# A planner's clock set to measured durations, and a DeltaNet front that may start beside the norm of the block two before

## The chip, the cores and the metric

The kernel runs on one core of a Trainium2 chip. The metric is the device time of one execution in microseconds, from start to end on that core; lower is better. Times of a profile come from one execution taken by the hardware profiler.

## The reference, cut to what matters

One layer of a hybrid encoder for two request groups with the same weights: a new stream of 16 meta tokens and 1024 frames, and a running stream of 64 frames. D_MODEL is 2048, and everything is float32.

```python
xn = _rmsnorm(h, norm_w)
proj = jnp.einsum('bld,dp->blp', xn, w_in)                 # 2048 x 8208
a_b, a_c, a_x, a_z, qkv, z_b, b_logit, a_logit = jnp.split(proj, PROJ_CUTS, axis=-1)
u_full = jnp.concatenate([conv_a_prev.astype(dt), a_c * a_x], axis=1)
y_a = a_b * _causal_conv(u_full, conv_a_w) * jax.nn.silu(a_z)          # mixer A, width 3
qkv_c = jax.nn.silu(_causal_conv(qkv_full, conv_qkv_w)).astype(f32)    # mixer B, width 4
# q, k normalised per head (8 heads of 128); beta = sigmoid(b); g = -exp(a_log) * softplus(a + dt_bias)
# gated delta rule in chunks, exact WY form:
a_mat = jnp.where(strict, kk, 0.0) + eye
t_mat = lax.linalg.triangular_solve(a_mat, eye, left_side=True, lower=True, unit_diagonal=True)
v_new = u_i - w_i @ s;  o = q_i exp(g_i) @ s + qk_i @ v_new;  s = s exp(g_last) + k_i.T @ v_new
o = _rmsnorm(o, o_norm_w) * jax.nn.silu(z_b)
y = jnp.einsum('blm,md->bld', jnp.concatenate([y_a, y_b], axis=-1), w_out)   # 2048 x 2048
return h + y                                               # then a final rmsnorm
```

## The kernel before, in words

**Tiles and stages.** The 1104 tokens lie in three pieces of 336, 384 and 384 columns (`PIECES`), and 9 chunks of 128 columns for the delta rule, three in a piece. A float32 product is three passes of the one-pass type `fp32r`: the tensor and the weight are each split into a high and a low part (`xh`, `xl`, `wh`, `wl`), and high times high, low times high and high times low are summed in PSUM. ScalarE makes `wh` (a cast), VectorE makes `wl` (a subtraction).

- Up to about 250 us: the input is loaded, normed and split while the first jobs run.
- To about 1843 us: the **jobs**. A job (`project`, line 427 and on) is 128 columns of `w_in` for all three pieces: 16 steps of k, each nine matmuls of 320 to 384 columns, into three of the four PSUM buffers `pj`. Weights come in four chunks of four k (`Weights.get`). After each k it calls `pump`. When a job is done, `post` has VectorE read its PSUM out (`raw`, `cs`, `xt`, `za`, `ya`, `zr`) and puts the rest of its convolution in a queue, `convs`. The jobs of a head of mixer B are k, q, v, z; of mixer A c, x, z, b. They come in the order b0 b1 b2 b3 a2 b4 a3 b5 a4 b6 b7 a5 a6 a7, after a0 and a1.
- Beside the jobs: the **DeltaNet** blocks, 24 of them (8 heads, 3 pieces; `NG`). `dn_front` (line 772) loads `kq`, transposes q and k (`psq`, `psk`), norms them, makes the masks `bm` and `at`, multiplies (`psm`, one for each chunk), and hands `bm` to GpSimd, which inverts 32x32 triangles in a loop of 60 instructions and returns them through DRAM in `t32` (in the trace `t`). `dn_back` (line 858) completes the inverse (`psx`, `psy`), then for each of the three chunks forms `r`, `u` and the new state (`psr`, `psu`, `psn`, `po`), then norms the output (`so`, `ro`, `on`), transposes it (`pot`) and gates it (`zg`). The small matmuls are float32, two instructions each.
- From 1843 us: `w_out`, in blocks of 512 columns (`po`), residual, norm, stores.

**What sets the order.** VectorE's and TensorE's instructions go out in the order in which the program writes them, apart from matmuls that the framework moves forward where a PSUM buffer isn't free in its own estimate. The program finds the order with a clock of its own, `clk`, in planned microseconds: `mm` and `tr` add to `pe`, and the wrapper `Timed` (line 46) adds to `dve` and `act`, from whichever is later, TensorE's clock or the engine's own. A generator's `yield d` makes its next step due at the largest of the three clocks plus `d` (`step`, line 174); `pump` (line 183) runs every due step, one front and one back at a time, and then lets convolution steps out while VectorE's clock is less than 0.7 ahead:

```python
        while convs and clk["dve"] - clk["pe"] < 0.7:
            if not step(convs[0]):
                convs.popleft()
```

`flush_convs` writes out what is left of them at the end of a job, before `post`. A front starts when the one before is done and `f - b <= 1`, where `b` counts finished backs; a back starts when `el_done` of its block, the planned end of GpSimd's solve, is reached. The front sets that at its end:

```python
        pool_free[0] = el_done[3 * h + p] = max(clk["pe"] + EL[0], pool_free[0]) + EL[1]
```

In the back, the loop over chunks (line 911 and on) ends with `yield 0.2`; the norm follows in the same step as the end of the loop, then `yield 3.2`, then `pot` and `zg`. Before the last job (line 1047 and on) the program runs `pump` without matmuls until all 24 backs are done.

SP's queue issues the loads and most stores, in program order: weights (`Weights.load`, line 232), `kq` (line 776), `bm` to DRAM (line 841).

Of the kernel before, what the change touches and what calls it, by code (L numbers as in the profile page):

```python
# [8 lines left out]
F32 = mybir.dt.float32  # L9
# [8 lines left out]
P = 128  # L18
# [7 lines left out]
NG = 3 * NH  # L26
# [40 lines left out]
def hymba_kernel(ctx: ExitStack, tc: tile.TileContext, hT, x_prompt, x_sample, w_in, w_ba, w_out, cst1, cst2, par,  # L67
                 s_delta, fnw, y_p, y_s, o_ca, o_cq, o_dp, o_ds):
    nc = tc.nc
    clk = {"pe": 0.0, "dve": 0.0, "act": 0.0}  # L70
    V = Timed(nc.vector, clk, "dve", 0.09, 0.00104)
    S = Timed(nc.scalar, clk, "act", 0.2, 0.00083)
    G, T, Q = nc.gpsimd, nc.tensor, nc.sync

    def mm(out, lhsT, rhs, start, stop):
        n = 1
        for d in rhs.shape[1:]:
            n *= d
        if lhsT.dtype == F32R:
            clk["pe"] += max(n / 2400 + 0.003, 0.107)  # L80
        else:
            clk["pe"] += 4 * max(n, lhsT.shape[1]) / 2400
        T.matmul(out, lhsT, rhs, start=start, stop=stop)  # L83

    def tr(out, in_, idn):
# [53 lines left out]
    def rsqrt(y, t, v):  # L139

        V.tensor_scalar(t.bitcast(I32), v.bitcast(I32), 1, None, ALU.logical_shift_right)
        V.tensor_scalar(y.bitcast(I32), t.bitcast(I32), -1, 0x5F3759DF, ALU.mult, ALU.add)
        for _ in range(3):
            V.tensor_tensor(t, y, y, ALU.mult)
            V.scalar_tensor_tensor(t, t, -0.5, v, ALU.mult, ALU.mult)
            V.scalar_tensor_tensor(y, t, 1.5, y, ALU.add, ALU.mult)

# [20 lines left out]
    gens = []  # L168
    done = set()
    fronts, backs, el_done, front_of, state = [0], [0], {}, {}, {}  # L170
    running = {}
    pool_free = [0.0]

    def step(it):

        try:
            d = next(it[1])
        except StopIteration:
            return False
        it[0] = max(clk.values()) + (d or 0.0)  # L180
        return True

    def pump():
        while True:
            moved = False
            f, b = fronts[0], backs[0]
            if "gate" in done and "front" not in running and f < NG and f - b <= 1:
                h, p = divmod(f, 3)
                if (KQ, h, p) in done and (QQ, h, p) in done:
                    running["front"] = [0.0, dn_front(h, p)]  # L190
            if "back" not in running and b < f and b < NG and el_done.get(b, 1e9) <= clk["pe"]:
                h, p = divmod(b, 3)
                if (VQ, h, p) in done and (ZQ, h, p) in done:
                    running["back"] = [0.0, dn_back(h, p)]
            for k in list(running):
                if running[k][0] <= clk["pe"]:
                    moved = True
                    if not step(running[k]):
                        del running[k]
                        if k == "back":  # L200
                            backs[0] += 1
                        elif k == "front":
                            fronts[0] += 1
            if not moved:
                break
# [3 lines that stand above are left out]
# [6 lines left out]
    class Weights:  # L215
# [20 lines left out]
        def split(self):  # L236
# [5 lines left out]
            wl = self.room(self.n_split, "l")  # L242
            V.tensor_tensor(wl, wr, wh.bitcast(F32), ALU.subtract)
            self.out.append((wh, wl))
# [209 lines left out]
    with ExitStack() as pro:  # L454
# [80 lines left out]
        a, n = PIECES[0]  # L535
# [108 lines left out]
    with ExitStack() as pro:  # L644
# [10 lines left out]
        for p in range(3):  # L655
            a, n = PIECES[p]
# [99 lines left out]
    dn = net.enter_context(tc.tile_pool(name="dn", bufs=1))  # L756
# [3 lines left out]
    def tmp(name, tag, bufs, shape=(P, 3, P)):  # L760
        return dn.tile(list(shape), F32, tag=tag, name=name, bufs=bufs)

    def psd(name):
        return pd.tile([P, 4, P], F32, tag="pd", name=name)

    EL = (5.0, 45.0)
    t32 = [dn.tile([P, 3, P], F32, tag=f"t32_{i}", name=f"t32_{i}") for i in range(2)]
    for i in range(2):
        V.memset(t32[i], 0.0)
# [2 lines left out]
    def dn_front(h, p):  # L772

        kq = tmp("kq", "kq", 2, (P, 3, 2, P))
        for i, w in ((0, KQ), (1, QQ)):
            Q.dma_start(kq[:, :, i, :], scr[h][w][p].rearrange("p (c t) -> p c t", t=P))
        gr = tmp("gr", "gr", 1)
        r0 = h * NCH + 3 * p
        Q.dma_start(gr, gscr[None, r0:r0 + 3, :].to_broadcast([P, 3, P]))
        yield 2.1  # L780
        c3 = slice(3 * p, 3 * p + 3)
        ss = dn.tile([P, 6], F32, tag="ss", name="ss", bufs=2)
        jk = dn.tile([P, P], BF16, tag="jk", name="jk")
        pq_ = psd("psq")
        for c in range(3):
            tr(pq_[:, c, :], kq[:, c, 1, :], ident)
        for c in range(3):
            S.activation(jk, pq_[:, c, :], AF.Square, accum_out=ss[:, 3 + c:4 + c])
        yield 0.0
        pk_ = psd("psk")  # L790
        for c in range(3):
            tr(pk_[:, c, :], kq[:, c, 0, :], ident)
        for c in range(3):
            S.activation(jk, pk_[:, c, :], AF.Square, accum_out=ss[:, c:c + 1])
        V.tensor_scalar(ss, ss, 4 * EPS, None, ALU.add)
        rq = rsqrt_of(dn, ss, 6, "rq")


        cq = dn.tile([P, 12], F32, tag="cq", name="cq", bufs=2)
        V.tensor_scalar(cq[:, 0:3], rq[:, 3:6], float(P) ** -0.5, None, ALU.mult)  # L800
        V.tensor_tensor(cq[:, 3:6], hb[:, h, c3], rq[:, 0:3], ALU.mult)
        V.tensor_tensor(rq[:, 3:6], rq[:, 0:3], rq[:, 0:3], ALU.mult)
        V.tensor_tensor(cq[:, 6:9], nbeg[:, h, c3], rq[:, 3:6], ALU.mult)
        V.tensor_tensor(cq[:, 9:12], nb[:, h, c3], rq[:, 3:6], ALU.mult)
        kn = tmp("kn", "kn", 2)
        V.tensor_tensor(kn, pk_[:, 0:3, :], kds[:, h, c3, None].to_broadcast([P, 3, P]), ALU.mult)
        km = None
        if p == 0:
            km = dn.tile([P, P], F32, tag="km", name="km")
            V.tensor_scalar(km, pk_[:, 0, :], kdm[:, h:h + 1], None, ALU.mult)  # L810
        yield 0.0

        bm = tmp("bm", "bm", 2)
        for c in range(3):
            cc = 3 * p + c
            V.scalar_tensor_tensor(bm[:, c, :], gr[:, c, :], gc[:, h, cc:cc + 1], cst[:, C_MS:C_MS + P], ALU.subtract,
                                   ALU.max)
        S.activation(bm, bm, AF.Exp, scale=-1.0)
        at = tmp("at", "at", 2)
        for c in range(3):  # L820
            cc = 3 * p + c
            V.scalar_tensor_tensor(at[:, c, :], gr[:, c, :], gc[:, h, cc:cc + 1], cst[:, C_MT:C_MT + P], ALU.subtract,
                                   ALU.min)
        S.activation(at, at, AF.Exp)
        S.activation(gr, gr, AF.Exp)
        if p == 0:

            V.memset(bm[64:P, 0, 0:64], 0.0)
            V.memset(at[0:64, 0, 64:P], 0.0)
        yield 0.0  # L830
        for c in range(3):
            pm = psd("psm")
            mm(pm[:, 0:2, :], kq[:, c, 0, :], kq[:, c, :, :], True, True)
            V.scalar_tensor_tensor(bm[:, c, :], pm[:, 0, :], cq[:, 9 + c:10 + c], bm[:, c, :], ALU.mult, ALU.mult)
            V.tensor_tensor(at[:, c, :], pm[:, 1, :], at[:, c, :], ALU.mult)
            yield 0.0
        yield 1.4

        eT = dn.tile([12, 32, 32], F32, tag="eT", name="eT", bufs=1)
        i = (3 * h + p) % 2  # L840
        Q.dma_start(whole(e_in[i]), bm)
        G.dma_start(eT, blocks(e_in[i]))  # L842
        tm = dn.tile([12, 240], F32, tag="tm", name="tm", bufs=1)
        for j in range(1, 31):
            n = 31 - j
            t = tm[:, 0:n * j].rearrange("m (i r) -> m i r", r=j)
            G.tensor_tensor(t, eT[:, j + 1:32, j:j + 1].to_broadcast([12, n, j]),  # L847
                            eT[:, j:j + 1, 0:j].to_broadcast([12, n, j]), ALU.mult)
            G.tensor_tensor(eT[:, j + 1:32, 0:j], eT[:, j + 1:32, 0:j], t, ALU.add)  # L849
        G.dma_start(blocks(e_out[i]), eT)  # L850
        G.dma_start(t32[i], whole(e_out[i]))
        yield 0.3

        V.tensor_tensor(kq[:, :, 1, :], kq[:, :, 1, :], gr, ALU.mult)
        front_of[h, p] = (kq, kn, km, at, cq, bm)
        pool_free[0] = el_done[3 * h + p] = max(clk["pe"] + EL[0], pool_free[0]) + EL[1]

    def dn_back(h, p):
        kq, kn, km, at, cq, bm = front_of.pop((h, p))
# [51 lines left out]
        for c in range(3):  # L911
# [31 lines left out]
            mm(po[:, c, :], kq[:, c, 1, :], s, False, True)  # L943
            state[h] = sn
            yield 0.2
        if p == 2:
            Q.dma_start(o_dp[h], state[h])

# [308 lines left out]
```

## Time and profile before

| | us |
|---|---|
| median of 3 runs | 2252.47 (2252.29 to 2257.59) |
| the profiled execution | 2251.76 |
| its span, first to last instruction | 2250.0 |
| TensorE busy | 2188.0 |
| VectorE busy | 1361.8 |
| GpSimd busy | 875.4 |
| ScalarE busy | 602.4 |

The granted clock of TensorE was 0.994 of full speed over the span. A busy time counts instructions that run, without waits for semaphores; ends of matmuls are modelled by the profiler. "Idle before" is the time for which an engine stood ahead of a group of instructions, and the name behind it is what ended that.

### The profile page before, as it was taken

How to read it: one execution, taken by the hardware profiler on the slowest of the kernel's cores; microseconds unless marked ns; L12 is line 12 of the kernel's file. 1: busy time of each engine (PE TensorE's matmuls, PEld its weight loads, DVE VectorE, ACT ScalarE, POOL GpSimd, SP SyncE). 2: the span in 40 equal slices, each digit the busy share in tenths (PEclk: the TensorE clock that was granted, in tenths of full speed). 3: DMA queues.
4: the chain of work that ended last, by engine and by line, in shares of the span. 5: the costliest groups of instructions: out<-in, count | busy, mean ns of one | idle time of the engine just before them, and what ended most of it. 6: DMA issues, size and time to landing. Idle time of an engine off the chain costs nothing. (4 is left out here: it accounts for less than half of the span.)

```text
span 2250.0 us, 35424 instructions
## 1 busy us (share of the span) xinstructions
PE 2188.0 (97%) x12794; PEld 2071.4 (92%) x12794; DVE 1361.8 (61%) x3540; ACT 602.4 (27%) x1483; POOL 875.4 (39%) x1516
## 2 busy tenths in 40 slices
PE   8999999999999999999999999999999999999997
PEld 8999899999999999999999999999999997788886
DVE  6653475777585556665775567675645345474644
ACT  7232121222222212212222222222221125444341
POOL 0000038475556566666657655657473000000000
PEclk9999999999999999999999999999999999999999
DMA  7223132222222122223232223232221228664652
GB/s 262 78 87 94 39 92 81 84 86 89 84 88 81 56 81 88 81 59 90 72 99 64 81 75 87 85 87 78 72 74 53 94 82 279 207 198 145 225 166 85
DMA packets 162067, 231.12 MB, mean 103 GB/s; under 512 B 17756, under 2 KB 89636, under 8 KB 161764
## 3 DMA queue, kind: packets, MB, share of 16 engines
q1 hardware_dynamic: 156356, 217.30, 31.2%
q0 software_dynamic: 3072, 7.11, 1.7%
q10 hardware_dynamic: 2464, 4.46, 0.5%
q8 instruction: 100, 1.64, 0.3%
q14 instruction: 75, 0.61, 0.1%
HBM read 184.61 MB, written 44.17 MB: 102 GB/s over the span
## 5 line engine op out<-in xcount | busy, mean ns | idle before, releaser
L83 PE MATMUL pj<-xh,wh 128*128 128x384 f32 x2048 | 694.9, 340 | 11.5 <-DVE raw L61 3.9
L83 PE MATMUL pj<-xl,wh 128*128 128x384 f32 x2048 | 692.4, 338 | 1.3 <-DVE xl L61 1.3
L83 PE MATMUL pj<-xh,wl 128*128 128x384 f32 x2048 | 691.3, 338 | 0.0
L61 DVE TENSOR_TENSOR wl<-wr,wh 128x512 fp32r<-128x512 f32 x464 | 335.5, 725 | 343.6 <-ACT wh L61 341.0
L83 PE MATMUL pj<-x,wh 128*128 128x320 f32 (+3 forms) x2048 | 519.2, 333 | 6.6 <-ACT x L61 6.6
L61 ACT CAST wh<-wr 128x512 fp32r<-128x512 f32 x464 | 285.8, 618 | 845.5 <-PE pj L83 626.7
L847 POOL TENSOR_TENSOR tm<-eT 12x30 f32<-12x30 f32 (+4 forms) x720 | 399.6, 555 | 121.7 <-DMA eT<-e_in 67.1
L849 POOL TENSOR_TENSOR eT<-eT,tm 12x30 f32<-12x30 f32 (+4 forms) x720 | 422.9, 587 | 56.4
L83 PEld LDWEIGHTS pj<-xh,wh 128*128 128x128 f32 x2048 | 387.2, 189 | 17.3 <-DVE xt L61 4.8
L83 PEld LDWEIGHTS pj<-xl,wh 128*128 128x128 f32 x2048 | 387.0, 189 | 2.9 <-DVE xl L61 2.2
L83 PEld LDWEIGHTS pj<-xh,wl 128*128 128x128 f32 x2048 | 386.8, 189 | 0.0
L83 PEld LDWEIGHTS pj<-x,wh 128*128 128x128 f32 x2048 | 349.3, 190 | 12.6 <-ACT x L61 6.7
L83 PE MATMUL pj<-x,wl 128*128 128x320 f32 (+3 forms) x1024 | 320.4, 313 | 5.2 <-DVE wl L61 5.2
L842 POOL DMA_DIRECT2D eT<-e_in x24 | 17.2, 716 | 578.2 <-DMA wr<-in_w_in 310.8
L83 PE MATMUL po<-wh,yh 128*128 128x512 f32 x656 | 238.9, 396 | 1.6 <-DVE yh L61 1.5
L83 PE MATMUL po<-wl,yh 128*128 128x512 f32 x528 | 208.9, 396 | 1.8 <-DVE wl L61 1.7
L83 PEld LDWEIGHTS pj<-x,wl 128*128 128x128 f32 x1024 | 193.3, 189 | 7.1 <-DVE wl L61 6.6
L83 PEld LDWEIGHTS po<-wh,yh 128*128 128x128 f32 x656 | 123.1, 188 | 32.9 <-DVE yh L61 2.7
L61 DVE SCALAR_TENSOR_TENSOR acc<-raw,pk,acc 128x384 f32<-128x384 f32 (+1 forms) x216 | 147.1, 681 | 6.0
L83 PE MATMUL po<-wh,yl 128*128 128x512 f32 x336 | 132.8, 395 | 0.0
L83 PEld LDWEIGHTS po<-wl,yh 128*128 128x128 f32 x528 | 99.1, 188 | 27.5 <-DVE wl L61 4.0
L61 ACT ACTIVATE raw<-acc 128x384 f32<-128x384 f32 (+1 forms) x72 | 36.8, 512 | 154.2 <-DVE acc L61 154.2
(242 smaller groups left out, 2127.9 us busy)
## 6 DMA issues: line engine op xcount, KB each, us to landing
wr<-in_w_in SPq DMA_DIRECT2D x288, 256.0 KB, 3.1
wr<-in_w_out SPq DMA_DIRECT2D x176, 256.0 KB, 2.8
scr<-acc SPq DMA_DIRECT2D x48, 192.0 KB, 1.9
kq<-scr SPq DMA_DIRECT2D x48, 192.0 KB, 3.0
hres<-in_x_prompt SPq DMA_DIRECT2D x32, 256.0 KB, 5.4
yr<-yscr SPq DMA_DIRECT2D x32, 192.0 KB, 3.7
scr<-co SPq DMA_DIRECT2D x24, 192.0 KB, 2.4
gr<-gscr SPq DMA_DIRECT2D x24, 192.0 KB, 3.5
```

What stands on the lines that cost most here:

```text
L61: return fn(out, *a, **k)
L83: T.matmul(out, lhsT, rhs, start=start, stop=stop)
L842: G.dma_start(eT, blocks(e_in[i]))
L847: G.tensor_tensor(t, eT[:, j + 1:32, j:j + 1].to_broadcast([12, n, j]), eT[:, j:j + 1, 0:j].to_broadcast([12, n, j]), ALU.mult)
L849: G.tensor_tensor(eT[:, j + 1:32, 0:j], eT[:, j + 1:32, 0:j], t, ALU.add)
```

## The change

Six edits. VectorE's charge for an instruction rises from 0.09 to 0.19 planned us. TensorE's charge for an `fp32r` matmul of n columns goes from n/2400 + 0.003 to 0.000453 n; for float32 from four times n/2400 (at least 128 columns) to twice 0.00086 n, at least 0.107 each. `EL` goes from 5 + 45 to 4 + 48. A new counter, `freed`, counts backs that are through their third chunk, and a front may start when it is at most one ahead of that counter, where it was the count of finished backs. `cq` gets a third buffer, because a front may now write its own while the norm of the block two before still reads one.

```diff
-    V = Timed(nc.vector, clk, "dve", 0.09, 0.00104)
+    V = Timed(nc.vector, clk, "dve", 0.19, 0.00104)
...
         if lhsT.dtype == F32R:
-            clk["pe"] += max(n / 2400 + 0.003, 0.107)
+            clk["pe"] += max(n * 0.000453, 0.107)
         else:
-            clk["pe"] += 4 * max(n, lhsT.shape[1]) / 2400
+            clk["pe"] += 2 * max(n * 0.00086, 0.107)
...
+    freed = [0]
...
-            if "gate" in done and "front" not in running and f < NG and f - b <= 1:
+            if "gate" in done and "front" not in running and f < NG and f - freed[0] <= 1:
...
-    EL = (5.0, 45.0)
+    EL = (4.0, 48.0)
...
-        cq = dn.tile([P, 12], F32, tag="cq", name="cq", bufs=2)
+        cq = dn.tile([P, 12], F32, tag="cq", name="cq", bufs=3)
...
             state[h] = sn
             yield 0.2
+        freed[0] += 1
         if p == 2:
             Q.dma_start(o_dp[h], state[h])
```

## Rows read from the trace of the kernel before

**Rows 1.** Page, part 1; then busy time by engine of one stretch.
```profile
PE 2188.0 (97%) x12794; PEld 2071.4 (92%) x12794; DVE 1361.8 (61%) x3540; ACT 602.4 (27%) x1483; POOL 875.4 (39%) x1516
...
core 0: us, PE busy (x) PEld busy (x) DVE busy (x) ACT busy (x) POOL busy (x), PEclk, DMA share, GB/s
250.00:1843.00 1593.00, 1557.73 (x9699) 1529.07 (x9697) 997.58 (x2774) 348.12 (x996) 875.21 (x1512) 0.99 0.27 78
```

**Rows 2.** Waits of TensorE: line waited for, us in total, times, longest.
```profile
PE pot L87 <- DVE on L61: 8.9, 4, 2.9
...
PE pj L83 <- DVE wl L61: 5.2, 4, 2.1
PE pj L83 <- DVE raw L61: 3.9, 4, 2.0
PE pj L83 <- DVE cs L61: 3.6, 3, 1.3
PE psx L83 <- DVE b L61: 3.2, 3, 1.3
PE pj L83 <- DVE xt L61: 3.1, 5, 0.9
PE psu L83 <- DVE r L61: 2.3, 4, 0.8
PE psy L83 <- ACT x L61: 2.0, 2, 1.3
...
PE psm L83 <- DVE kn L61: 1.4, 2, 0.7
...
PE psr L83 <- ACT sn L61: 1.3, 1, 1.3
```

**Rows 3.** The chain that ended last: start us, us, what.
```profile
1762.09 80.99 PE pj L83 x489
...
1915.31 287.98 PE po L83 x1233
```

**Rows 4.** VectorE by shape: names, shapes, count; busy us, mean ns; idle before.
```profile
L61 DVE TENSOR_TENSOR wl<-wr,wh 128x512 fp32r<-128x512 f32 x464 | 335.5, 725 | 343.6 <-ACT wh L61 341.0 <-PE po L83 1.0
L61 DVE SCALAR_TENSOR_TENSOR acc<-raw,pk,acc 128x384 f32<-128x384 f32 x144 | 101.2, 703 | 3.9
...
L61 DVE SCALAR_TENSOR_TENSOR rot<-rot,so 128x3 f32<-128x3 f32 x72 | 20.2, 281 | 2.5
...
L61 DVE TENSOR_TENSOR t<-t,cst 128x384 f32<-128x384 f32 x24 | 14.1, 589 | 0.0
...
L61 DVE TENSOR_TENSOR rqt<-rqy 128x6 f32<-128x6 f32 x72 | 12.7, 176 | 2.5
```

**Rows 5.** Timeline, 570 to 579 us: start, us, instruction, idle before and its end.
```profile
571.01 0.39 PE L83 MATMUL po<-sn,kq 128*128 128x128 f32 x2
...
572.64 0.16 DVE L61 TENSOR_TENSOR so<-so,cq 128x3 f32<-128x3 f32 x1 [1.30 <-ACT jk L61]
...
577.37 0.56 DVE L61 TENSOR_TENSOR on<-po,roy 128x384 f32<-128x384 f32 x1
...
577.98 0.90 PE L87 MATMUL pot<-cst,on 128*128 128x128 f32 x3 [2.92 <-DVE on L61]
```

**Rows 6.** Timeline at a job change near 1371 us.
```profile
1370.82 0.57 DVE L61 TENSOR_TENSOR raw<-pj,rs 128x256 f32<-128x256 f32 x3
...
1371.53 0.41 PE L83 MATMUL pj<-xh,wh 128*128 128x384 f32 x1 [1.98 <-DVE raw L61]
```

**Rows 7.** SP's waits; then instructions, with first and last start in us.
```profile
SPq L776 <- PE po L83: 21.5, 10, 4.4
...
L87 PE MATMUL psq<-cst,kq x9: 272/272/273, 1242.9 to 1359.3; 128*128 128x128 f32 x9
...
L87 PE MATMUL pot<-cst,on x72: 270/272/474, 410.2 to 1761.8; 128*128 128x128 f32 x72
```

**Rows 8.** Busy times of two stretches, each one front's norm (columns as in rows 1).
```profile
1184.30:1189.05 4.75, 4.75 (x30) 4.75 (x29) 4.20 (x19) 0.69 (x2) 4.09 (x9) 1.00 0.00 0
1364.70:1368.24 3.54, 3.54 (x23) 3.43 (x22) 3.00 (x18) 0.68 (x2) 0.78 (x1) 1.00 0.54 159
```

## The prediction, made before the changed kernel ran

> **What bounds the kernel now.** I read the busy shares first: TensorE is busy for 2188.0 of 2250.0 us, every other engine for 61% or less [rows 1]. So the end is set by how long TensorE takes, and only two things can move it: the work of TensorE, which the change leaves as it is (the same matmuls, in the same steps), and the time in which TensorE stands. In the stretch that holds all DeltaNet steps, 250 to 1843 us, it stands for 1593.00 - 1557.73 = 35.3 us [rows 1]. The second view is the list of what TensorE waited for [rows 2]. It splits into three kinds. **DeltaNet waits:** 8.9 for the normed output `on` before the transpose `pot`, 3.2 before `psx`, 2.3 before `psu`, 2.0 before `psy`, 1.4 before `psm`, 1.3 before `psr`: 19.1 us. **Job changes:** 3.9 + 3.6 + 3.1 = 10.6 us, in which the next projection has no PSUM until VectorE has read the last one out (`raw`, `cs`, `xt`). **Split weights:** 5.2 us for `wl`. All three end on VectorE, which is not full (61%): it is late, not short of time. Together 34.9 us, 1.5% of the span, and that is the most which a better order can give.
>
> **Why VectorE is late: the plan undercharges it.** The program lays out its order with a clock of its own. A step of a DeltaNet generator becomes ready at the largest of three engine clocks plus its yield, and is written out when TensorE's clock gets there. A yield that is too short, or a VectorE clock that is too slow, therefore puts a matmul in TensorE's strict order ahead of its operand. Old and new charges against the trace:
> - TensorE, 512 columns: old 512/2400 + 0.003 = 0.216 us, new 0.232. The chain has 1233 such matmuls in 287.98 us, 0.2336 each [rows 3]. Projection: 489 matmuls, a third with 320 columns or so, in 80.99 us, 0.1656 each [rows 3]; old charge (2 x 0.163 + 0.136)/3 = 0.154, new (2 x 0.174 + 0.145)/3 = 0.164. The old clock ran some 7% fast, so a yield of 1 us lasted 1.07 us of real matmuls; the new one is right. By itself this shortens every cover by 7%.
> - VectorE, 128x512: old 0.62, new 0.722, measured 725 ns. Three elements: old 0.093, new 0.193, measured 176 to 281 ns [rows 4]. So 0.1 us more for each instruction. This lengthens every cover behind many small instructions.
>
> **The worst wait, worked through.** Behind the third chunk of a block the norm issues 15 tiny VectorE instructions and `on`. In one block the last `po` matmul starts at 571.01, VectorE's chain runs from 572.64 to 577.37 + 0.56 = 577.93, and `pot` waits 2.92 us [rows 5]: 6.5 us were needed from the end of `po` (571.4). Old plan: 15 x 0.093 + 0.49 + yield 3.2 = 5.1 plan us, 5.5 real. New: 15 x 0.193 + 0.59 + 3.2 = 6.7 us, and rounded up to the next group of nine matmuls (9 x 0.1656 = 1.5 us). 6.7 covers 6.5, just.
>
> **Part by part.**
> - *`pot`.* Of 8.9 us I take 8 off, by the sum above. Bounds: 8.9 off, and nothing.
> - *Other DeltaNet waits,* 10.2 us. Their yields (0.25 to 1.05) get 7% shorter; what they gain is that VectorE's clock now holds the backlog of convolution steps. Two multiply-adds were charged 0.98 us, now 1.18. I take half, 5 us off; bounds 10.2 off and 5 added (half again).
> - *Job changes,* 10.6 us. At one of them VectorE still runs the front's norm (17 small instructions, `kn` and `km`, then `bm` and `at`) until 1370.82, where it begins to read out, and TensorE restarts at 1371.53 after 1.98 us [rows 6]. With the new charges (17 x 0.195 = 3.3 us against 1.6) `bm` and `at` are written one or two groups later, behind the read-out. I take 3 off; bounds 10.6 off and 8 added (the same wait of 1.98 at four more changes).
> - *`wl`,* 5.2 us: the same cause; 2 off, bounds 5.2 off and 2 added.
> - *The front beside norm and gate.* The next front is now released when the third chunk is done, not after `pot` and the gate. Its loads of `kq` go to SP's queue right behind that block's last matmuls; already now such a load waits for `po` 10 times, 21.5 us in all [rows 7], with weight loads queued behind it, and behind those ScalarE's casts. The front's `psq` then stands about 1.1 plan us ahead of `pot` (3.5 + 2.1 against 3.5 + 3.2) instead of 3 behind. Its VectorE instructions stay behind `on` in program order, so the norm isn't delayed by them; the gate's `zg` may be. I take 3 us added, bounds 0 and 8. `cq` with a third buffer is 48 bytes a partition: nothing.
> - *`EL`,* 4 + 48 for 5 + 45: the back may start 52 us after the front instead of 50 x 1.07 = 53.5. The solved blocks are in time today: VectorE's `t` never waits [rows 4], and 1.5 us less doesn't use that up in most blocks. Taken at nothing; a late one stops VectorE's queue for as long as it is late, and this is inside the 8 us of the part before.
> - *DeltaNet's own pace.* Two blocks are in flight, and a pair takes 116.4 us (`psq` of one front to that of the next but one) [rows 7]. A front has 31 VectorE instructions and a back 29, so some 3 us more in each; the earlier release gives back about 4, `EL` 1.5. The pace stays, give or take 4 us a pair. Cover: the last `pot` is at 1761.8 [rows 7], and the program waits for DeltaNet only before the last job, 144 matmuls from the end of the projections at 1843.1, so at 1843.1 - 144 x 0.1656 = 1819 [rows 3]. The slack is 57 us.
> - *The output projection and the tail* have no DeltaNet step; their steps cost one group of matmuls each before and after. Nothing.
>
> Sum against the profiled execution (2251.76 us, of it 2250.0 span): 2251.8 - 8 - 5 - 3 - 2 + 3 = 2236.8. The median of the runs is 0.7 us above that execution; I take 2237.
>
> **A rule that speaks against one flat charge.** The same chain of a front (17 tiny instructions, `kn`, `km`) took 4.20 us of VectorE in a stretch in which GpSimd was busy for 4.09 of 4.75 us, and 3.00 us in one in which GpSimd had 0.78 of 3.54 [rows 8]. (The first stretch has one instruction more at its end.) The Trainium skill, SBUF — State Buffer, "SBUF: two separate sides", says that VectorE and GpSimd share one port pair as an exclusive lock, and that a VectorE instruction with two SBUF inputs and a GpSimd instruction that reads SBUF hold each other up for a whole instruction. By that rule the trace agrees. What it makes of the change is the first rival.
>
> **Rivals.**
> 1. *The flat 0.19 is too little while GpSimd solves.* The norm needs 6.5 us and gets 6.7; a solve that runs through it, with the other front's chain now beside it, uses that up. Then `pot` gives back 4 instead of 8, the other DeltaNet waits 3 instead of 5: 2251.8 - 4 - 3 - 3 - 2 + 3 = 2243. For it: the 1.2 us between the two stretches. Against it: the rounding up to a group of 1.5 us. Chance 0.15.
> 2. *The waits move to the job changes.* Steps are put off in a plan that is as full as before; what TensorE no longer waits for at `pot` it waits for when PSUM is to be read out. Half of the 18 us is lost again, and job changes gain nothing: about 2250. This is also the case that the plan moves and TensorE ends alike. For it: some 43 of the 56 job changes lie beside the 24 blocks. Chance 0.18.
> 3. *Slower: convolution steps are left over at the end of a job.* They are written out only while VectorE's clock is less than 0.7 us ahead of TensorE's, and what is left goes out at once ahead of the read-out. A q, k or v job is charged some 2.9 (splits) + 3.9 (read-outs) + 9.3 (taps) + 17.6 x 25/58 = 7.6 (DeltaNet) = 23.7 us of about 25, against 17 before. It decides where that passes the job's TensorE time. Price: one step of two multiply-adds (2 x 0.70 us [rows 4]) at some 21 such jobs, 29 us: 2237 + 29 = 2266. Against it: that work lies ahead of the read-out in either order, and the new charge is close to the measured one. Chance 0.10.
> 4. *DeltaNet outlives the projections.* At over 57/11 = 5 us more a pair the last back runs without cover. At 8 us: 31 us stand, 2237 + 31 = 2268. Chance 0.07.
>
> **How the numbers follow.** The forecast itself (2226 to 2246) has 0.50. What a measurement tells from no change is about 0.3%, 6.8 us: 2245.7 and 2259.2 are the bounds. Faster: 0.47 of the forecast, 0.10 of the first rival, 0.03 of the second: 0.60. Slower: the third and fourth, less a part of them that ends inside: 0.15. Same: 0.25. The range goes from 2221 (nearly all of the 34.9 us back) to 2262 (into the third rival).
>
> **What would show it.** Right: `pot <- DVE on` under 1.5 us among TensorE's waits, DeltaNet waits together near 6, TensorE's idle time in the projections down from 35 to some 20 us, last `pot` within 40 us of 1761.8. First rival: `pot` keeps 4 us or more. Second: `raw`, `cs`, `xt` over 15 us. Third: the same with runs of `acc` just ahead of the read-outs. Fourth: `psx`, `psu` and `psr` waits of several us after 1819. The forecast is wrong if new waits appear that VectorE doesn't end: SP's loads of weights, or `t` behind GpSimd.

## The result, and the profile after

| | before | after |
|---|---|---|
| median, us | 2252.45 | 2282.57 (2276.98 to 2285.42) |
| ratio to before, 95% interval | | 1.0125 [1.0111, 1.014] |
| the profiled execution: time, span | 2251.76, 2250.0 | 2276.98, 2275.2 |
| TensorE busy | 2188.0 | 2195.1 |
| first matmul of the gate's projection | 237.1 | 241.3 |
| last transpose `pot` | 1761.8 | 1824.1 |

The change makes the kernel 1.25% slower, where 0.7% faster was forecast. It issues the same 12794 matmuls. The profiled execution is the fastest of its runs; its span is 25.2 us longer.

The waits of TensorE after the change (as in [rows 2]: what waited for what, us in total, times, longest):

```profile
PE pj L83 <- DVE raw L61: 15.7, 8, 3.5
PE pj L83 <- DVE zr L61: 10.3, 4, 4.9
PE psm L83 <- DVE km L61: 7.1, 2, 3.8
...
PE psm L83 <- DVE kn L61: 5.6, 4, 2.3
PE pj L83 <- DVE wl L61: 5.3, 5, 1.4
PE pj L83 <- DVE xt L61: 3.1, 4, 1.4
...
PE pj L83 <- DVE ya L61: 2.0, 2, 1.6
...
PE psq L87 <- DMA kq<-scr: 1.4, 1, 1.4
...
PE psu L83 <- DVE r L61: 0.9, 2, 0.7
```

`pot`, the longest of before (8.9 us), is not in the list any more, nor are `psx` (3.2) and `psr` (1.3). The waits have gone to the **job changes**: `raw` from 3.9 to 15.7, `zr` from nothing in the list to 10.3; and to `psm`, from 1.4 to 12.7. All waits of TensorE together rise from 51.1 to 68.9 us.

The busy shares (page, part 1, beside [rows 1]):

```profile
PE 2195.1 (96%) x12794; PEld 2078.5 (91%) x12794; DVE 1371.5 (60%) x3540; ACT 602.5 (26%) x1483; POOL 873.2 (38%) x1516
```

Busy times in the stretch of the projections, which now ends at 1868 us:

```profile
core 0: us, PE busy (x) PEld busy (x) DVE busy (x) ACT busy (x) POOL busy (x), PEclk, DMA share, GB/s
250.00:1868.00 1618.00, 1566.38 (x9723) 1537.12 (x9722) 1010.04 (x2781) 348.89 (x999) 873.03 (x1512) 0.99 0.27 77
```

TensorE stands for 80.1 us of the span instead of 62.0 (18.1 more), and the same matmuls are busy for 7.1 us more: together the 25.2 us. In the projections it stands for 51.6 us instead of 35.3.

What a job change looks like now. The timeline of VectorE and TensorE from 1492 us (start, us, instruction, idle before and what ended it):

```profile
1492.51 0.56 DVE L61 TENSOR_TENSOR ti<-ti,psy 128x384 f32<-128x384 f32 x1 [3.37 <-PE psy L83]
...
1493.40 1.67 DVE L61 SCALAR_TENSOR_TENSOR acc<-raw,pk,acc 128x384 f32<-128x384 f32 x2
...
1495.66 0.77 DVE L61 SCALAR_TENSOR_TENSOR acc<-raw,acc 128x384 f32<-128x384 f32 x1 [0.59 <-ACT raw L61]
...
1496.36 0.69 DVE L61 TENSOR_SCALAR acc<-raw,pk 128x384 f32<-128x384 f32 x1
1497.08 2.49 DVE L61 SCALAR_TENSOR_TENSOR acc<-raw,pk,acc 128x384 f32<-128x384 f32 x3
...
1500.16 0.93 DVE L61 SCALAR_TENSOR_TENSOR acc<-raw,acc 128x384 f32<-128x384 f32 x1 [0.59 <-ACT raw L61]
1501.01 0.62 DVE L61 TENSOR_TENSOR raw<-pj,rs 128x256 f32<-128x256 f32 x3
...
1501.69 0.69 PE L83 MATMUL pj<-xh,wh 128*128 128x384 f32 x1 [3.50 <-DVE raw L61]
```

VectorE first stands idle for 3.37 us, although eight convolution instructions are waiting to be written out. They stand behind the DeltaNet step `ti` in its order, because the plan held them back. Then they come in one run, from 1493.4 to 1501, and only behind them comes the read-out that frees PSUM. TensorE stands for 3.50 us.

How often this happens can be counted in VectorE's order in the trace: the convolution instructions that stand directly ahead of the first read-out of a job, from 290 to 1850 us. **Before, none at any of 54 job changes. After, at 17 of 53, one to eight instructions each, 48.6 us of VectorE.** Below these are called left-over steps.

The same order tells what every wait at a job change stands behind: TensorE's waits that end from 1 us before to 4.5 us after the first read-out begins, put down to the VectorE instruction directly ahead of that read-out (290 to 1850 us). Together they are 25.9 us before and 44.1 after. Of the 44.1 us, 24.9 stand behind left-over steps, and 14.2 behind the norm of a front (`kn` or `km`, at 8 changes; before, 1.4 us at 2), most of it under the name `psm`. Behind `bm` and `at` it is 1.4 us (8.4 before), behind a block's norm `on` 3.2 (8.7 before).

### The profile page after: what moved, and what is told of

Same layout as the page of the kernel before. It is cut to its first block, busy times and chain, and to the rows that moved or that the text cites. A ratio compares the mean times of both kernels' runs of the same rounds, so it can differ in the third digit from the quotient of the medians.

```text
span 2275.2 us, 35428 instructions
## 1 busy us (share of the span) xinstructions
PE 2195.1 (96%) x12794; PEld 2078.5 (91%) x12794; DVE 1371.5 (60%) x3540; ACT 602.5 (26%) x1483; POOL 873.2 (38%) x1516
## 4 chain that ended last, share of the span: by engine, by line
PE 85%; DVE 9%; ACT 2%; issue 1%; DMA 1%; SPq 0%; DVEq 0%; ACTq 0%
PE pj L83 60%; PE po L83 17%; DVE acc L61 3%; PE psy L83 1%; PE psx L83 1%; PE psm L83 1%; ACT jk L61 1%; DVE rqt L61 1%; PE pjb L83 1%; PE psn L83 1%; PE psu L83 1%; PE psr L83 1%; DVE wl L61 1%; DVE rqy L61 1%; DVE rot L61 0%
## 5 line engine op out<-in xcount | busy, mean ns | idle before, releaser
L83 PE MATMUL pj<-xh,wh 128*128 128x384 f32 x2048 | 698.7, 342 | 31.5 <-DVE raw L61 15.7
L83 PE MATMUL pj<-x,wh 128*128 128x320 f32 (+3 forms) x2048 | 513.4, 331 | 6.6 <-ACT x L61 6.4
L61 DVE SCALAR_TENSOR_TENSOR acc<-raw,pk,acc 128x384 f32<-128x384 f32 (+1 forms) x216 | 152.5, 706 | 6.0
```

The costliest lines, as they stand in the source:

```text
L61: return fn(out, *a, **k)
```

## The experiments

Theory A: VectorE's larger charge fills the plan, convolution steps are held back, and the left-over ones go out ahead of the read-out. Theory B: the early release of the front crowds VectorE. Theory C: TensorE's larger charge makes every cover 7% shorter. Of the columns, "left over" is the count of above (job changes with such steps, us), "read-outs" are TensorE's waits for `raw`, `zr`, `cs`, `xt`, `za` and `ya` together.

| kernel | us | ratio to before | left over | read-outs, us | wait for `pot` | last `pot` |
|---|---|---|---|---|---|---|
| before | 2252.5 | | 0, 0 | 11.5 | 8.9 | 1761.8 |
| after | 2282.6 | 1.0125 [1.0111, 1.014] | 17, 48.6 | 31.4 | 0 | 1824.1 |
| e1_vec | 2366.2 | 1.0502 [1.0487, 1.0518] | 21, 51.7 | 45.3 | 24.0 | 1935.4 |
| e1_rel | 2256.5 | 1.0017 [1.0007, 1.0026] | 3, 2.9 | 10.1 | 3.9 | 1756.5 |
| e1_pe | 2270.9 | 1.0075 [1.0051, 1.0099] | 1, 0.9 | 9.2 | 12.8 | 1761.6 |
| e2_novec | 2257.5 | 1.0014 [1.0004, 1.0025] | 2, 1.1 | 13.4 | 4.6 | 1745.0 |
| e4_v14 | 2259.1 | 1.0020 [1.001, 1.0031] | 9, 14.7 | 13.0 | 7.1 | 1765.3 |
| e2_th3 | 2307.2 | 1.0243 [1.0225, 1.0261] | 4, 5.7 | 13.0 | 12.3 | 1878.2 |
| e3_drain | 2263.6 | 1.0045 [1.003, 1.0059] | 1, 0.6 | 19.6 | 0 | 1816.1 |
| e3_norel | 2315.5 | 1.0277 [1.0257, 1.0297] | 19, 45.3 | 38.8 | 13.3 | 1888.3 |
| e3_split | 2251.5 | 0.9994 [0.9983, 1.0005] | 7, 16.6 | 15.2 | 5.2 | 1759.6 |
| e4_bsplit | 2258.0 | 1.0020 [1.001, 1.003] | 7, 24.1 | 25.0 | 0.5 | 1828.6 |
| e4_splitdrain | 2251.7 | 0.9989 [0.9978, 1.0001] | 0, 0 | 10.6 | 0 | 1760.4 |
| e4_y48 | 2245.7 | 0.9965 [0.9952, 0.9978] | 1, 0.7 | 11.7 | 0 | 1774.2 |
| e5_pe_rel | 2271.6 | 1.0064 [1.0044, 1.0083] | 4, 5.1 | 11.8 | 5.0 | 1755.4 |
| e5_pe_y48 | 2276.5 | 1.0099 [1.0075, 1.0123] | 0, 0 | 15.9 | 8.2 | 1779.3 |
| e6_pe_el | 2256.8 | 1.0021 [1.0011, 1.0031] | 1, 0.8 | 15.3 | 6.4 | 1757.2 |
| e6_y48_el | 2258.6 | 1.0030 [1.0017, 1.0043] | 2, 2.8 | 13.6 | 3.9 | 1810.8 |

### Which of the edits costs the time

e1_vec, VectorE's charge alone (with the one more edit behind all DeltaNet blocks that its expectation names):
```diff
-    V = Timed(nc.vector, clk, "dve", 0.09, 0.00104)
+    V = Timed(nc.vector, clk, "dve", 0.19, 0.00104)
```


> The kernel before with one edit of the six: VectorE's charge 0.19 instead of 0.09. (So that the program can still be laid out, what is left of the convolution steps of the last job is written out at the eleventh step of the first block of w_out; that touches one place after all DeltaNet blocks.) Theory A, the charge holds convolution steps back, and they go out in one piece at the end of a job ahead of the read-out: as slow as the whole change or slower, 2275 to 2295 us, with the waits for raw and zr at job changes at 20 us or more and the wait for pot gone. Theory B, the front beside the norm crowds VectorE: no loss here, 2235 to 2250. Theory C, the larger charge for TensorE shortens the covers: no loss here either.

Far slower than expected, 2366. The left-over steps are there (21 job changes, 51.7 us); the wait for `pot` isn't gone but 24.0 us. More is added: with TensorE's old, fast clock and the late release the DeltaNet blocks fall so far behind that they outlive the projections. The longest waits of TensorE:

```profile
PE psx L83 <- DVE b L61: 28.4, 2, 27.0
PE pot L87 <- DVE on L61: 24.0, 8, 7.0
PE pj L83 <- DVE raw L61: 19.2, 12, 6.3
PE pj L83 <- DVE zr L61: 17.8, 4, 5.7
```

Busy times in the stretch ahead of the last job (columns as in [rows 1]):

```profile
1875.00:1960.00 85.00, 39.63 (x181) 34.61 (x181) 21.71 (x63) 9.26 (x30) 24.75 (x47) 0.62 0.18 54
```

In 85 us TensorE is busy for 39.6, at a granted clock of 0.62: it waits 27.0 us for one solved block. So this kernel loses by the third rival of the prediction and the fourth at once.

e1_rel, the early release alone (`freed`, and `cq` with three buffers, as in the change).


> The kernel before with the early release of the front alone (the counter of backs that are through their third chunk, and the third cq). Theory A: within 5 us of before, 2247 to 2258. Theory B: most of the 25 to 30 us is here, 2270 or more, and the waits are for kn, km and pot.

4 us slower, and hardly a left-over step: Theory B has no more than that. SP's loads of `kq` cost it 3.8 us at `psq`.

e2_novec, the change with VectorE's charge back at 0.09:
```diff
-    V = Timed(nc.vector, clk, "dve", 0.19, 0.00104)
+    V = Timed(nc.vector, clk, "dve", 0.09, 0.00104)
```


> The changed kernel with VectorE's charge back at 0.09; the charges of TensorE, the early release and EL stay changed. Theory A: the loss is gone, 2245 to 2260, no convolution step in front of a read-out, and the wait for pot is back. Theory B or C: the loss stays, 2270 to 2285.

Of the 30 us 25 are gone, the left-over steps too (1.1 us), and `pot` waits again (4.6 us). That is Theory A: **the other five edits together cost 0.14%, VectorE's charge in their company 1.1%.**

e4_v14, the change with the charge at 0.14.


> The changed kernel with VectorE's charge at 0.14, halfway between 0.09 (2257) and 0.19 (2283). Theory A with its point of decision, that steps are left over only once the charges of a job pass its TensorE time: few left-over steps, and nearer to the lower end, 2250 to 2265. If the loss grows evenly with the charge: 2265 to 2275 and half of the 49 us of left-over steps.

2259.1, at the lower end. Half of the charge brings 0.06% of the 1.11%, so the loss isn't even. But the left-over steps are not few, as Theory A expected: 14.7 us at 9 job changes. TensorE's waits behind them are 8.6 us, while those behind `bm` and `at` are 0.5 instead of 8.4, so the two make up for each other. That the loss begins where the plan is full is argued.

### Are the left-over steps the cause, or only beside it?

e3_drain, the change with the left-over steps taken away without touching any charge; in `project`, behind `pump`:
```diff
                     pump()
+                    if k >= 8 and convs and not step(convs[0]):
+                        convs.popleft()
```


> The changed kernel in which, in the last eight k of a job, one waiting convolution step goes out after each k whatever VectorE's clock says; charges and DeltaNet steps as changed. Theory A (the loss comes from steps that are left to the end of a job and stand ahead of the read-out): hardly any convolution instruction directly ahead of a read-out, waits for raw and zr under 8 us instead of 26, time 2248 to 2265. Rival D (the larger charge costs time by slowing the DeltaNet steps, and the left-over steps are harmless): 2272 to 2290, and the last pot later than 1823.8.

The left-over steps are gone (0.6 us), the read-outs wait 19.6 us instead of 31.4, and 19 of the 30 us come back by the medians. So they are the cause of about two thirds. In the profiled executions, the fastest of the changed kernel and the slowest of this one, it is 8.1 us: the waits at job changes fall from 44.1 to 29.4, but `wl` rises from 5.3 to 9.3 and `psu` from 0.9 to 3.6. The forecast of under 8 us for `raw` and `zr` was too good (13.3): at all of these waits but one of 1.5 us a DeltaNet instruction (`kn`, `at`, `on` and the like) now stands directly ahead of the read-out. The last third isn't settled by this run; some 5 us of it lie ahead of the gate, whose projection begins at 241.9 us here, and the norm of a front still stands ahead of 7 read-outs (11.1 us).

e2_th3, the same end by a wider throttle:
```diff
-        while convs and clk["dve"] - clk["pe"] < 0.7:
+        while convs and clk["dve"] - clk["pe"] < 3.0:
```


> The changed kernel in which convolution steps go out while VectorE's clock is less than 3.0 ahead of TensorE's (0.7 in both kernels); all charges as changed. Theory A: fewer steps are left at the end of a job, so the waits for raw and zr fall from 26 us to 10 or less, and the time to 2240 to 2262. Theories B and C: convolution steps crowd the DeltaNet steps all the more, 2275 or more.

The left-over steps go (5.7 us) and the waits for read-outs with them (13.0), as Theory A has it, but the time rises to 2307. A DeltaNet step is due only when TensorE's clock has reached VectorE's; with VectorE's up to 3 us ahead, each of the 24 steps of a block comes later, the last `pot` is at 1878, and blocks run without cover. The throttle of 0.7 is what gives DeltaNet its pace.

e3_norel, the change without the early release.


> The changed kernel without the early release (a front starts after the back of the block two before is done, cq with two buffers); all charges as changed. Theory A: the loss stays, 2270 to 2300; DeltaNet has some 4 us a pair less and its last pot comes 30 to 60 us later than 1823.8, so it may run past the projections. Theory B (the early release crowds VectorE): the loss goes, 2260 or less.

2315.5, above the range: the release is worth 33 us in this company, probably because it wins back the pace that the charge costs. Without it the last `pot` is at 1888 and the projections end at 1909, so that only the last job, some 20 us, is left behind it: the last block ran without cover. TensorE waits 13.3 us for `pot`, 4.8 of it at that block. Theory B is wrong in its sign.

### Only the DeltaNet steps charged more

e3_split: the change, but in `pump` VectorE is charged 0.19 while a front or back is stepped and 0.09 otherwise:
```diff
-                    if not step(running[k]):
+                    V._f = 0.19 if k in ("front", "back") else 0.09
+                    more = step(running[k])
+                    V._f = 0.09
+                    if not more:
```


> The changed kernel with VectorE charged 0.19 inside the DeltaNet generators only, and 0.09 in convolutions, splits and read-outs. Theory A: the convolution steps fit the plan again, none or few are left over; the longer covers of the DeltaNet steps stay, so the wait for pot is under 2 us and the time 2238 to 2256, below the 2257 of the kernel with 0.09 throughout. Rival D: DeltaNet steps are as slow as in the changed kernel, 2270 or more.

e4_bsplit, the same edit on the kernel before:


> The kernel before with VectorE charged 0.19 inside the DeltaNet generators only; TensorE's charges, EL and the release as before. Theory A: DeltaNet's pace is slower by some 5 us a pair without the early release, still inside its slack, and the covers are longer: 2240 to 2256. Theory F (DeltaNet outlives the projections as in the kernel with all of VectorE at 0.19): over 2270, and the last pot after 1830.

e4_splitdrain, e3_split with the drain of e3_drain:


> The kernel of e3_split (0.19 in DeltaNet generators only) with the drain of e3_drain (one waiting convolution step after each of the last eight k). Theory A: the 17 us of left-over steps that e3_split still has go, and with them most of its 12.6 us of waits for raw and zr: 2238 to 2250. Rival E: 2250 to 2262.

All three end within 0.2% of before, and each misses part of its forecast: e3_split still has left-over steps (16.6 us) and 5.2 us for `pot`, e4_bsplit is above 2256, and e4_splitdrain lands where Rival E put it. The 31 us between e3_split and the changed kernel are the price of the charge outside the DeltaNet steps. The waits behind the left-over steps of e3_split and e4_bsplit (10.3 and 10.6 us) are again made up for by those behind `bm` and `at` (0.5 and none, 8.4 before). With the drain no step is left over and `pot` never waits, yet `wl` waits 8.9 us and `psu` 5.4: of what one place gave back most was lost at others. e4_bsplit shows how near DeltaNet is to its limit: its last `pot` is 67 us later than before.

### The term for `pot` by itself

e4_y48, the kernel before with one number changed:
```diff
-        yield 3.2
+        yield 4.8
```


> The kernel before with one number changed: the yield between the norm and pot is 4.8 instead of 3.2, so pot gets the cover that the larger charge gave it, and nothing else in the plan grows. The prediction's term for pot by itself: the 8.9 us of that wait go, 2240 to 2248. Rival E (a wait that is taken off one place comes back at the next, since VectorE is late by the same amount of work): 2249 to 2256, pot's wait gone all the same.

**2245.7, ratio 0.9965 [0.9952, 0.9978]: 0.35% faster than before, clear of noise.** The waits of TensorE:

```profile
PE pj L83 <- ACT x L61: 6.5, 1, 6.5
PE pj L83 <- DVE wl L61: 5.3, 5, 2.1
PE pj L83 <- DVE raw L61: 3.8, 4, 2.0
PE psm L83 <- DVE kn L61: 3.0, 3, 2.1
PE pj L83 <- DVE zr L61: 2.8, 1, 2.8
```

`pot` isn't in its list, and nothing has taken its place in full: 46.4 us together instead of 51.1, so 4.2 of the 8.9 us are back elsewhere. At three job changes a block's norm `on` still stands directly ahead of the read-out, as at three before; TensorE waits 5.1 us there, now under `zr`, `za` and `cs`. By the ratio of the runs the gain is the 8 us of the term, and it needed none of the charges; the profiled execution, one of the slower runs, is 1.8 us under that of before.

### TensorE's charge

e1_pe, the two charges of `mm` alone.


> The kernel before with TensorE's charges alone changed (0.000453 n, and 2 times 0.00086 n). Its clock runs 7% further for each matmul, so there is more room for VectorE in the plan and every yield lasts shorter. Theory A: no left-over steps; 2248 to 2262. Theory C (shorter covers cost the time): 2265 or more, with the waits for pot, psx, psu and psy above the 17 us of before.

18 us slower, as Theory C had it, with hardly a left-over step and 12.8 us for `pot` instead of 8.9. Two runs were to tell whether it is the shorter covers.

e5_pe_rel, with the early release:


> The kernel before with TensorE's charges and the early release (third cq), nothing else. If the early release is what takes the 18 us of e1_pe away: 2252 to 2262. If the covers made 7% shorter are what costs: 2264 to 2275, as e1_pe.

e5_pe_y48, with the yield of 4.8:


> The kernel before with TensorE's charges and the yield before pot at 4.8. If shorter covers are what costs in e1_pe: the 12.8 us of pot's wait go, 2252 to 2262. If not: 2264 or more although pot no longer waits.

Neither takes it off. The second is inconclusive on its own question, because `pot` still waits 8.2 us with the longer yield; what TensorE waits for most is split weights (`wl`, 20.2 us). What these three share is a wait of VectorE that before and after don't have (from e5_pe_rel, VectorE's waits):

```profile
DVE t L61 <- DMA t<-e_out: 4.2, 1, 4.2
```

With TensorE's clock right and `EL` at 5 + 45, one to three of the 24 backs start before GpSimd's block is there (2.0 us in 3 in e1_pe). Hence two more:

e6_pe_el, TensorE's charges and `EL`:


> The kernel before with TensorE's charges and EL at 4 + 48. If the loss of TensorE's charges is that the back starts before GpSimd's block is back, so that VectorE stops at t: no wait at t, and 2252 to 2262. If it is only how the steps happen to fall: anywhere from 2255 to 2280.

e6_y48_el, `EL` and the yield of 4.8, TensorE's clock as before:


> The kernel before with the yield before pot at 4.8 and EL at 4 + 48 (2 planned us more between front and back; TensorE's clock as before). VectorE has no wait at t there to lose, so EL gives nothing: within 4 us of the kernel with the yield alone, 2242 to 2250. If a later back is a gain by itself: 2240 or less.

With `EL` TensorE's charges cost 4 us instead of 18, as forecast, but not for the reason that was tested. The wait at `t` is still there (e6_pe_el, VectorE's waits):

```profile
DVE t L61 <- DMA t<-e_out: 3.7, 2, 2.4
```

It is longer than the 2.0 us of e1_pe, so it isn't what cost the 14 us. That leaves the other reading of the expectation, how the steps happen to fall; what cost them stays open. `EL` beside the longer yield cost 13 us, where nothing was expected, and there VectorE never waits for `t`. In the traces most of it lies at the job changes: TensorE's waits there are 29.1 us against 17.3 in e4_y48, and a norm (`on`, `kn` or `km`) stands directly ahead of 13 first read-outs instead of 7 (22.6 us against 9.8). So a few planned us in one place move the norms onto the job changes or off them. Among kernels with hardly a left-over step the ratios go from 0.9965 to 1.0099, a spread as large as the loss of the change; a difference of some tenths of a per cent between two of these kernels doesn't by itself show what its edit was meant to show.

## Why the prediction was wrong, point by point

**`pot`: right in size, partly by luck.** 8 of 8.9 us were to go; all went, and e4_y48 measures the term alone at 0.35%. But the sum doesn't give the wait that it was held against: 6.5 us needed and 5.5 given leave 1.0 us, and `pot` waited 2.92 ([rows 5]). There TensorE stood at `pot` from 575.06, only 3.7 us behind the end of the last `po`. A job ends in that place; directly behind `on` VectorE begins its read-out (timeline of VectorE, before):

```profile
577.84 0.94 DVE L61 TENSOR_TENSOR zr<-pj,rs 128x320 f32<-128x320 f32 x2
```

The three long waits for `pot` before, 8.7 of the 8.9 us, all stand like this. So they were waits at job changes as well as of DeltaNet, and a longer cover moves part of them to the read-out (5.1 us in e4_y48). That `pot` was moved forward there, past matmuls without PSUM, is argued. The first rival (the flat charge is too little while GpSimd solves) fell: `pot` does not wait once.

**Other DeltaNet waits: right in part.** `psx`, `psu`, `psy` and `psr` fell from 8.8 to 1.4 us, more than the half that was taken. But `psm` rose from 1.4 to 12.7, all of it at six job changes without a left-over step. At a job change the framework moves `psm` forward, since no PSUM is free for the next projection, and TensorE then stands there instead of at the read-out:

```profile
849.25 1.03 PE L83 MATMUL psm<-kq 128*128 128x256 f32 x4
853.63 0.67 PE L83 MATMUL psm<-kq 128*128 128x256 f32 x2 [3.36 <-DVE km L61]
```

VectorE writes `km` at 853.15 and begins the read-out at 853.41, so in this place it is the lateness of the read-out, behind the front's norm, under another name. It is what the prediction saw at 1371 us and expected to shrink.

**Job changes: this is the step that failed.** The prediction took 3 us off 10.6 and set 8 added as the worst. Measured: the read-outs went from 11.5 to 31.4 us, and all waits at job changes, under whatever name, from 25.9 to 44.1. The reasoning held for `bm` and `at`, which do move behind the read-out (directly ahead of it at 4 changes instead of 14). It missed the front's norm itself, which now stands there at 8 changes (14.2 us), and above all the convolution steps, which it had in hand (17 changes, 24.9 us).

**The third rival was the case, and its chance was wrong.** It named the mechanism and its point, "where that passes the job's TensorE time", and had the charges of a q, k or v job at 23.7 of about 25 us. It got 0.10 on the argument that the same work lies ahead of the read-out in either order. That is what the timeline at 1492 us refutes: the work isn't done earlier, because the plan holds the steps back while VectorE stands idle for 3.37 us ahead of a DeltaNet step. That an average of 23.7 in 25 hides jobs which hold a whole front is argued, not shown. Its price was 29 us (21 jobs, one step each); it came as 17 job changes with up to eight instructions, 48.6 us of VectorE; of the 30 us of the end e3_drain gives back 19. e4_v14 fits the point: with half the charge nearly nothing is lost.

**DeltaNet's pace: right in kind, just past its edge.** A pair was to keep 116.4 us "give or take 4"; here it takes 120.8, and the last `pot` comes 62 us later, 12 of them already at the first block (422.2 against 410.2):

```profile
L87 PE MATMUL psq<-cst,kq x9: 271/272/273, 1285.7 to 1406.5; 128*128 128x128 f32 x9
...
L87 PE MATMUL pot<-cst,on x72: 270/272/273, 422.2 to 1824.1; 128*128 128x128 f32 x72
```

The slack of 57 us is used up but for some 20. The fourth rival did not decide here; it did in e1_vec, e2_th3 and e3_norel.

**The front beside norm and gate: right.** 3 us were added for SP's loads of `kq`; e1_rel measures 4 us for the whole edit. (Beside the larger charge it gains 33, e3_norel.) SP now waits 37.8 us in 15 places for `po` with those loads, 21.5 in 10 before ([rows 7]), and TensorE 1.4 us for one of them.

**`EL` at nothing: not measured by itself in the change.** VectorE never waits for `t` after the change. Beside other edits `EL` moved the end by 14 us down (e1_pe to e6_pe_el) and 13 up (e4_y48 to e6_y48_el), which the prediction didn't see.

**Left out: the start.** The larger charge also delays the norm of the input; the gate's projection begins at 241.3 instead of 237.1 us, 4 us of the 25. In the runs with VectorE at 0.09 it begins at 236.5 to 239.2.

**Left out: the clock.** A wait was priced at its own length. Of the 25.2 us 7.1 are the same matmuls running longer; more stretches at the lower clock fit that (last section).

## What to carry to other kernels

In a list order that is written ahead by a planner's clock, a cost that is right for each instruction can be wrong for the plan: it decides not only when a step is due but also which filler work is held back, and what is held back comes out in one piece at the worst place. Before raising a charge, add up the plan's load per stage at the new charges, for the fullest stage and not the mean, and follow what becomes of the filler when it doesn't fit. If the trace shows one late wait, lengthen that cover alone and measure: one yield gave 0.35%, where the right durations everywhere cost 1.25%, but the same yield beside another `EL` cost 0.30%. And before a wait is put down to the operand that ends it, look at what the late engine does next: if it goes on to free the buffers that the waiting engine needs for its other work, a longer cover may only change the name of the wait.

## What the runs showed of the hardware

After its longest waits TensorE ran at half speed for some time. It waits 4.91 us for `zr` and starts again at 348.18 (timeline of TensorE, after):

```profile
348.18 0.69 PE L83 MATMUL pj<-xh,wh 128*128 128x384 f32 x1 [4.91 <-DVE zr L61]
348.66 0.52 PE L83 MATMUL pj<-xl,wh 128*128 128x384 f32 x1
348.98 0.52 PE L83 MATMUL pj<-xh,wl 128*128 128x384 f32 x1
...
353.57 0.33 PE L83 MATMUL pj<-xh,wh 128*128 128x384 f32 x1
353.75 0.33 PE L83 MATMUL pj<-xl,wh 128*128 128x384 f32 x1
```

The stretches ahead of it, around it and behind it (columns as in [rows 1]; the granted clock is the third from the end):

```profile
330.00:342.00 12.00, 11.46 (x68) 11.01 (x66) 11.76 (x23) 2.50 (x5) 10.82 (x16) 1.00 0.09 24
342.00:354.00 12.00, 6.24 (x22) 6.01 (x23) 10.14 (x18) 2.55 (x5) 10.74 (x17) 0.72 0.42 122
354.00:366.00 12.00, 12.00 (x74) 12.00 (x73) 1.71 (x3) 1.24 (x2) 5.87 (x13) 1.00 0.40 99
```

From 348.2 to 353.4 us matmuls of 384 columns start every 0.32 us, from 353.6 on every 0.17: the two levels, 1.2 and 2.4 GHz. In 5.2 us TensorE did the work of 2.6, so this wait of 4.91 us cost 7.5, an estimate from these starts. The same shows behind the waits of 3.4 to 4.1 us that begin at about 701, 850, 1112, 1498 and 1590 us: the granted clock is 0.72 to 0.86 over 12 us around each. Shorter waits went either way. One of 1.84 us at 57 us was followed by a slow stretch (0.86 from 56 to 68 us); three of 2.2 to 2.3 us at 639, 1291 and 1468 us and those of 1.4 to 1.7 us at 667, 1381 and 1651 us were not (1.00). The kernel before has such stretches too, behind its three long waits for `pot` and behind waits of 2.1 us at 289 and 2.0 at 1370 us; around the second `pot`:

```profile
694.00:706.00 12.00, 9.09 (x40) 8.81 (x40) 8.13 (x21) 1.97 (x5) 10.40 (x21) 0.72 0.33 111
```

So what the change adds is the difference. The mean granted clock of the profiled execution is 0.994 before and 0.990 after; 0.004 of 2275 us is 9 us, an estimate that fits the 7.1 us by which the same matmuls are busy longer. No run separates it. It makes a few long waits dearer than their sum.
